# The scores of the RWKV scans: both banks claimed first, the products of the two heads in turn

## The chip, the cores and the metric

The kernel runs on one core of one Trainium2 chip. The metric is the time of one execution on the device, in microseconds (us); the median of three runs counts. A core has TensorE (matrix products, with results in the eight banks of PSUM), VectorE, ScalarE and GpSimd, and queues that issue DMAs.

## The reference

The reference is one inference step of a hybrid trunk: two layers (DEPTH = 2) over 512 latent and 128 context tokens, 1024 channels. Each layer has one input projection whose columns feed four parallel groups (RWKV-7 time mixing, retention, Mamba-2, differential attention), an output projection and a gated ConvFFN. The change lies in the RWKV group, 4 heads of 64 channels and two directions:

```python
def rwkv_scan(r, w, k, v, kk, a, s0):
    def step(s, inp):
        r_t, w_t, k_t, v_t, kk_t, a_t = inp
        sa = jnp.einsum('bhvk,bhk->bhv', s, -kk_t)
        s = s * w_t[:, :, None, :] + sa[..., None] * (kk_t * a_t)[:, :, None, :] + v_t[..., None] * k_t[:, :, None, :]
        return s, jnp.einsum('bhvk,bhk->bhv', s, r_t)
    ...
y_f, s_f = rwkv_scan(rh, hs(decay[:, :, 0]), k_f, vh, kk, hs(a_f), s0[:, 0])
y_b, s_b = rwkv_scan(flip_t(rh), flip_t(hs(decay[:, :, 1])), flip_t(k_b), flip_t(vh), flip_t(kk),
                     flip_t(hs(a_b)), s0[:, 1])
```

## The kernel before

Tokens are on the free axis (642 columns: 512 latent, a gap, 128 context), channels on the 128 partitions. Projections are float32r products in three parts (high and low halves), 48 products per 128 output channels.

The RWKV scan is computed in chunks of 64 tokens, ten in all (eight latent, two context). A tile of 128 channels holds two heads, on partitions 0 to 63 and 64 to 127, so each layer has four passes: tile t = 0, 1 and direction d = 0, 1. A pass has three stages.

- `rw_pre` builds the decayed vectors A and R (`A4`) and B and K (`B2`), and from them the scores: for each chunk e and head h, one product of 64 contraction rows, 128 by 128 in fp32 (line 575). The chunks come in three groups g of 4, 4 and 2 (`GRP`, line 447). A group takes one PSUM bank per head (`SMT`, line 573), so head h works on the row half 64h to 64h + 63 of the array and writes its own bank. VectorE then masks each bank out in two evictions, into `sca` (line 578) and `pk` (line 579), and four copies on ScalarE and GpSimd take the diagonal blocks into `AT` (line 584). `need(g)` (line 570) first drives the pass before until `pk`'s two buffers can be written again.
- `rw_sub` (line 622) inverts the chunks' triangles, a chain of short VectorE steps, with `rhs` (transposes `vt`, `bt`, products `rp`) between.
- `rw_solve` (line 698) makes `y`, the maps (`bg` on TensorE, read into `gq` by lines 732 to 736) and the sequential steps `st`.

Passes overlap: `rw_solve` of one pass runs beside `rw_pre` of the next (lines 1471 to 1484). The stages share four PSUM banks (`sbank`, line 120); a new tile takes a bank whose readers have finished. Projections (`p0r`, `gd` with its conv steps at lines 402 and 403, `rv`, `sx` and others) don't depend on the scan and stand in the same queues.

The order on each engine is not written out. A planner at build time walks all instructions once, with its own reckoning of their durations, and gives each engine at each moment the instruction that is earliest in the source among those whose inputs and tile are ready; on the chip each queue runs in that fixed order. `tc.high_priority` and `tc.issue_after` move a few blocks; none of them stands around the scores.

Further on, in the Mamba-2 group, two banks `pf` (`sf` in the trace) and `pi` (`si`) are claimed together (line 1121) and their products alternate in the source; then come the outputs of retention and attention, the output projection `po`, and the FFN (`pu`, `pd`).

Of the kernel before, what the change touches and what calls it, by code (L numbers as in the profile page):

```python
# [70 lines left out]
def tile_trunk(ctx: ExitStack, tc: tile.TileContext, xT, cT, wmod, win, wv1, wv2, wout, wup, wdn, wlora, gup, pp, srw,  # L71
# [9 lines left out]
    def mm(*a, **k):  # L81
        nonlocal last_pe
        last_pe = nc.tensor.matmul(*a, **k).ins  # L83
# [42 lines left out]
    def SMT(name):  # L126
        return sbank.tile(name)
# [29 lines left out]
    sc = keep.tile([128, KD, 32], F32, name="sc")  # L157
# [340 lines left out]
    def rw_pre(l, t, d, f, wa, rw, dv, S, need):  # L498

        nm = f"{l}_{t}_{d}"  # L500
# [66 lines left out]
        for g, ms in enumerate(GRP):  # L567
            nb = 2 * len(ms)
            n0 = 4 * g
            need(g)  # L570
            pk = rw.tile([128, 2 * len(GRP[g]), 2, 2, 64], F32, tag="pk2" if g == 2 else "pk", name=f"pk{nm}_{g}")
            for h in range(2):
                ps = SMT(f"sc{nm}_{g}_{h}")
                for e in range(nb):
                    mm(ps[:, 128 * e:128 * e + 128], lhsT=B2[64 * h:64 * h + 64, n0 + e, :],
                       rhs=A4[64 * h:64 * h + 64, :, n0 + e, :], start=True, stop=True)
                p4 = ps[:, 0:128 * nb].rearrange("p (e s c) -> p e s c", e=nb, s=2)
                vtt(sca[:, h, n0:n0 + nb], p4[:, :, 0, :], maskA.unsqueeze(1).to_broadcast([128, nb, 64]), MULT)
                vtt(pk[:, 0:nb, h, 1, :], p4[:, :, 1, :], maskR.unsqueeze(1).to_broadcast([128, nb, 64]), MULT)

            at = AT[:, n0:n0 + nb, :].rearrange("p (m h) c -> p h m c", h=2)
            for q in range(4):
                c0 = 32 * (q % 2)
                (nc.scalar.copy if q % 2 else nc.gpsimd.tensor_copy)(
                    at[32 * q:32 * q + 32], sca[32 * q:32 * q + 32, :, n0 + q // 2:n0 + nb:2, c0:c0 + 32])
            pks.append(pk)
            yield
# [786 lines left out]
    for l in range(DEPTH):  # L1374
# [28 lines left out]
        h = (hhi, hlo)  # L1403
# [20 lines left out]
        f = {}  # L1424
# [31 lines left out]
        def need(S_):  # L1456
            def upto(g):
                while S_["maps"] <= g:
                    pump(behind, 1)
            return upto  # L1460

        def pre(i):
            t, d = divmod(i, 2)
            if not d:
                if t:
                    fs[t] = rw_load(t)
                rw_prep(l, t, fs[t], dv, rw)
                yield
            yield from rw_pre(l, t, d, fs[t], wa, rw, dv, Ss[i + 1], need(Ss[i]))
# [414 lines left out]
```

## Time and profile before

| | us |
|---|---|
| median of three runs (2236.89 to 2243.23) | 2240.26 |
| the profiled execution | 2239.36 |
| its span, first to last instruction | 2237.6 |
| TensorE busy | 2098.0 (94%) |
| VectorE busy | 1312.9 (59%) |
| ScalarE busy | 815.2 (36%) |
| GpSimd busy | 275.6 (12%) |
| mean granted TensorE clock | 0.964 |

Engines are named PE (TensorE products), PEld (its weight loads), DVE (VectorE), ACT (ScalarE), POOL (GpSimd) and SP (a DMA queue). L83 is the helper that issues every product, so products are told apart by the tile that they write. An fp32 product has two records on PE. A record's end is modelled, and records of PE overlap: what a run of them costs is read from the starts. In a timeline, rows of the same kind are merged: start, time from the first start to the last end, and how many. The text in brackets is idle time just before, and what ended it.

### The profile page before, as it was taken

What the parts mean: (1) busy time and instruction counts of PE and PEld (TensorE: products, weight loads), DVE (VectorE), ACT (ScalarE), POOL (GpSimd) and SP (SyncE); (2) the same over time, 40 slices, a digit from 0 to 9 for tenths busy, and PEclk for the clock granted to TensorE, in tenths of its full rate; (3) what the DMA queues carried; (4) which work ended last, traced back from release to release, by engine and by line L of the source; (5) the groups of instructions that cost most, each with busy time, mean ns of one, the idle gap of its engine ahead of it and who ended that gap; (6) DMA issues with size and microseconds to landing.
All of it is one profiled execution on the core that took longest, in us unless ns stands there. A gap on an engine that the chain in (4) does not pass through costs nothing. (4 is left out here: it accounts for less than half of the span.)

```text
span 2237.6 us, 40813 instructions
## 1 busy us (share of the span) xinstructions
PE 2098.0 (94%) x16169; PEld 1908.4 (85%) x16169; DVE 1312.9 (59%) x2911; ACT 815.2 (36%) x1603; POOL 275.6 (12%) x460
## 2 busy tenths in 40 slices
PE   6999999987999999999989999999699999999997
PEld 3888887676889999999988888777578899999997
DVE  4787874546665535545457787656376654453553
ACT  4433432225553313323344334232264432232332
POOL 3112122310020000000121121222001100000002
PEclk9999997988999999999989999999799999999998
DMA  7212125664343422222321212265732222222221
GB/s 249 73 51 78 49 83 178 225 194 116 107 146 103 125 76 71 69 78 76 98 82 59 73 58 83 65 231 185 227 104 74 76 75 76 76 72 75 76 70 68
DMA packets 130943, 232.25 MB, mean 104 GB/s; under 512 B 14784, under 2 KB 34752, under 8 KB 130752
## 3 DMA queue, kind: packets, MB, share of 16 engines
q1 hardware_dynamic: 98304, 176.47, 26.3%
q10 hardware_dynamic: 32448, 53.17, 7.1%
q8 instruction: 128, 2.10, 0.4%
q14 instruction: 63, 0.52, 0.1%
HBM read 199.16 MB, written 30.42 MB: 103 GB/s over the span
## 5 line engine op out<-in xcount | busy, mean ns | idle before, releaser
L83 PE MATMUL pu<-hlo_n,wh_up 128*128 128x322 f32 (+1 forms) x1408 | 324.1, 310 | 1.0 <-POOL hlo_n L357 0.7
L83 PE MATMUL pu<-hhi_n,wh_up 128*128 128x322 f32 (+1 forms) x1408 | 323.8, 311 | 0.8 <-DVE gv L403 0.8
L83 PE MATMUL pu<-hhi_n,wl_up 128*128 128x322 f32 (+1 forms) x1408 | 323.6, 310 | 0.0
L184 DVE TENSOR_TENSOR wl_up<-wr_up,wh_up 128x512 fp32r<-128x512 f32 x176 | 124.7, 709 | 250.9 <-ACT wh_up L183 248.0
L83 PEld LDWEIGHTS pu<-hhi_n,wh_up 128*128 128x128 f32 x1408 | 236.8, 189 | 7.0 <-ACT gv L401 2.5
L83 PEld LDWEIGHTS pu<-hlo_n,wh_up 128*128 128x128 f32 x1408 | 236.9, 188 | 2.0 <-POOL hlo_n L357 1.4
L83 PEld LDWEIGHTS pu<-hhi_n,wl_up 128*128 128x128 f32 x1408 | 237.4, 189 | 0.0
L183 ACT CAST wh_up<-wr_up 128x512 fp32r<-128x512 f32 x176 | 108.3, 616 | 297.9 <-PE pu L83 254.0
L83 PE MATMUL pd<-gh,wl_dn 128*128 128x322 f32 x704 | 162.6, 312 | 0.0
L83 PE MATMUL pd<-gh,wh_dn 128*128 128x322 f32 x704 | 162.3, 312 | 0.0
L83 PE MATMUL pd<-gl,wh_dn 128*128 128x322 f32 x704 | 162.1, 311 | 0.0
L183 ACT CAST wh_dn<-wr_dn 128x512 fp32r<-128x512 f32 x96 | 56.0, 584 | 209.6 <-PE pd L83 168.1
L184 DVE TENSOR_TENSOR wl_dn<-wr_dn,wh_dn 128x512 fp32r<-128x512 f32 x96 | 61.9, 645 | 109.9 <-ACT wh_dn L183 109.3
L83 PEld LDWEIGHTS pd<-gh,wh_dn 128*128 128x128 f32 x704 | 119.5, 190 | 0.8 <-ACT gv L401 0.8
L83 PEld LDWEIGHTS pd<-gl,wh_dn 128*128 128x128 f32 x704 | 119.2, 190 | 0.3
L83 PEld LDWEIGHTS pd<-gh,wl_dn 128*128 128x128 f32 x704 | 119.1, 190 | 0.0
L410 DVE SCALAR_TENSOR_TENSOR x<-pd,mod,x 128x512 f32<-128x512 f32 x96 | 48.5, 547 | 93.7 <-PE pd L83 93.7
L83 PE MATMUL po<-ohi,wh_out 128*128 128x320 f32 (+1 forms) x256 | 77.3, 325 | 12.9 <-ACT ohi L198 12.8
L402 DVE SCALAR_TENSOR_TENSOR gv<-pu,pp,gv 128x641 f32<-128x641 f32 x88 | 77.9, 885 | 9.6 <-ACT gv L401 1.9
L403 DVE SCALAR_TENSOR_TENSOR gv<-pu,pp,gv 128x641 f32<-128x641 f32 x88 | 78.0, 887 | 3.2
L401 ACT ACTIVATE gv<-pu,pp 128x642 f32<-128x642 f32 x88 | 77.8, 884 | 0.0
L83 PE MATMUL po<-olo,wh_out 128*128 128x322 f32 (+1 forms) x256 | 77.7, 324 | 0.1
(741 smaller groups left out, 4477.4 us busy)
## 6 DMA issues: line engine op xcount, KB each, us to landing
wr_mod<-in_wmod SPq DMA_DIRECT2D x192, 256.0 KB, 4.8
wr_up<-in_wup SPq DMA_DIRECT2D x176, 256.0 KB, 2.6
wr_dn<-in_wdn SPq DMA_DIRECT2D x64, 256.0 KB, 2.7
wr_dn<-in_wdn SPq DMA_DIRECT2D x32, 192.0 KB, 2.3
olo<-scr_o ACTq DMA_DIRECT2D x16, 321.0 KB, 4.2
wr_out<-in_wout SPq DMA_DIRECT2D x16, 256.0 KB, 2.6
wr_out<-in_wout SPq DMA_DIRECT2D x32, 128.0 KB, 2.1
x_in<-in_xT SPq DMA_DIRECT2D x8, 321.0 KB, 5.7
```

The lines of the kernel that those rows point to most:

```text
L83: last_pe = nc.tensor.matmul(*a, **k).ins
L183: nc.scalar.copy(hi[:, :n], raw[:, :n])
L184: vtt(lo[:, :n], raw[:, :n], hi[:, :n].bitcast(F32), SUB)
L401: act(out, ps, AF.Identity, bias=0.0 if bias is None else bias, scale=wc)
L402: vstt(out[:, 1:T], ps[:, 0:T - 1], wl, out[:, 1:T], MULT, ADD)
L403: vstt(out[:, 0:T - 1], ps[:, 1:T], wr, out[:, 0:T - 1], MULT, ADD)
L410: vstt(xs, halves[0][:, c0:c0 + n], g[:, s:s + 1], xs, MULT, ADD)
```

## The change

Both banks of a group are claimed before its products, and the loops over chunks and heads change places, so that in the source the products of the two heads alternate. The evictions follow in a second loop over the heads, in the order of before. No product, eviction, bank or byte is added or removed.

```diff
             pk = rw.tile([128, 2 * len(GRP[g]), 2, 2, 64], F32, tag="pk2" if g == 2 else "pk", name=f"pk{nm}_{g}")
-            for h in range(2):
-                ps = SMT(f"sc{nm}_{g}_{h}")
-                for e in range(nb):
+            pss = [SMT(f"sc{nm}_{g}_{h}") for h in range(2)]
+            for e in range(nb):
+                for h, ps in enumerate(pss):
                     mm(ps[:, 128 * e:128 * e + 128], lhsT=B2[64 * h:64 * h + 64, n0 + e, :],
                        rhs=A4[64 * h:64 * h + 64, :, n0 + e, :], start=True, stop=True)
+            for h, ps in enumerate(pss):
                 p4 = ps[:, 0:128 * nb].rearrange("p (e s c) -> p e s c", e=nb, s=2)
                 vtt(sca[:, h, n0:n0 + nb], p4[:, :, 0, :], maskA.unsqueeze(1).to_broadcast([128, nb, 64]), MULT)
                 vtt(pk[:, 0:nb, h, 1, :], p4[:, :, 1, :], maskR.unsqueeze(1).to_broadcast([128, nb, 64]), MULT)
```

## Rows read from the trace of the kernel before

**Rows 1.** Stretches: PE, PEld, DVE, ACT, POOL busy (count), PEclk, DMA share, GB/s.

```profile
90.00:300.00 210.00, 203.04 (x2465) 178.50 (x2464) 169.74 (x577) 83.49 (x182) 34.35 (x109) 0.98 0.23 69
...
1191.00:1400.00 209.00, 202.30 (x2468) 177.47 (x2467) 169.19 (x569) 83.86 (x182) 34.70 (x109) 0.99 0.22 69
```

**Rows 2.** Timeline, layer 0, first pass: start, us, engine, line, operation, tiles, count.

```profile
91.78 3.60 PE L83 MATMUL sc<-AR,BK 64*128 64x128 f32 x40 [0.85 <-DVE BK L551]
...
92.36 0.87 DVE L402 SCALAR_TENSOR_TENSOR st_gd<-p0gd,d_muh,st_gd 64x641 f32<-64x641 f32 x1
...
93.16 0.41 DVE L578 TENSOR_TENSOR sca<-sc,cs 128x256 f32<-128x256 f32 x1
...
94.81 0.41 DVE L579 TENSOR_TENSOR pk<-sc,cs 128x256 f32<-128x256 f32 x1
...
95.37 0.96 PE L484 MATMUL vt<-cs,rwv 128*128 128x128 f32 x5
...
98.79 0.88 DVE L403 SCALAR_TENSOR_TENSOR st_gd<-p0gd,d_muh,st_gd 64x641 f32<-64x641 f32 x1
```

**Rows 3.** Timeline, layer 0, second pass, groups 0 and 1.

```profile
136.97 1.16 PE L83 MATMUL sc<-AR,BK 64*128 64x128 f32 x8
...
137.78 0.57 DVE L736 TENSOR_TENSOR gq<-bg,AR 64x128 f32<-64x128 f32 x2
...
138.06 0.39 PE L83 MATMUL rv<-wl_rv,hhi_n 128*128 128x264 f32 x1
...
138.74 1.16 PE L83 MATMUL sc<-AR,BK 64*128 64x128 f32 x8
...
140.37 1.95 PE L83 MATMUL bg<-pk,wx 128*128 128x128 f32 x16
```

**Rows 4.** Timeline of PE from 136.95 to 137.05 us alone.

```profile
136.77 0.28 PE L83 MATMUL bg<-pk,wx 128*128 128x128 f32 x1
136.97 0.37 PE L83 MATMUL sc<-AR,BK 64*128 64x128 f32 x1
```

**Rows 5.** Timeline, same pass, group 2: from 145.9 to 146.0 us alone, and whole.

```profile
145.95 0.39 PE L83 MATMUL sc<-AR,BK 64*128 64x128 f32 x2
...
145.95 0.72 PE L83 MATMUL sc<-AR,BK 64*128 64x128 f32 x8
```

**Rows 6.** Timeline, the pair sf and si of the Mamba-2 group, one instance.

```profile
445.11 0.49 PE L83 MATMUL sf<-css,gb 128*128 128x128 f32 x2
445.53 0.49 PE L83 MATMUL si<-ldsC,sst 64*128 64x128 f32 x2
```

**Rows 7.** Timeline, the same pair, the next instance.

```profile
452.72 0.49 PE L83 MATMUL sf<-css,gb 128*128 128x128 f32 x2
...
453.86 1.16 PE L83 MATMUL si<-ldsC,sst 64*128 64x128 f32 x8 [0.36 <-DVE rpt L952]
```

**Rows 8.** Timeline, layer 1, first pass.

```profile
1193.07 3.60 PE L83 MATMUL sc<-AR,BK 64*128 64x128 f32 x40 [0.72 <-DVE BK L551]
...
1196.66 0.96 PE L484 MATMUL vt<-cs,rwv 128*128 128x128 f32 x5
```

**Rows 9.** Timeline of PE, first and last sf of the same steps, both layers.

```profile
365.31 1.06 PE L83 MATMUL sf<-css,gb 128*128 128x128 f32 x4
...
378.21 0.41 PE L83 MATMUL sf<-css,gb 128*128 128x128 f32 x1
...
1465.28 1.06 PE L83 MATMUL sf<-css,gb 128*128 128x128 f32 x4
...
1473.42 0.38 PE L83 MATMUL sf<-css,gb 128*128 128x128 f32 x2
```

**Rows 10.** Stretches around these steps, columns as in rows 1.

```profile
360.00:370.00 10.00, 7.38 (x35) 6.14 (x34) 7.53 (x7) 2.57 (x6) 5.09 (x4) 0.75 0.72 258
370.00:380.00 10.00, 10.00 (x40) 9.05 (x40) 2.25 (x5) 2.27 (x8) 0.00 (x0) 0.50 0.36 109
...
1470.00:1480.00 10.00, 10.00 (x72) 9.29 (x75) 6.01 (x10) 4.52 (x12) 0.00 (x0) 1.00 0.52 157
```

## The prediction

> **What bounds the kernel now.** I read the stretches first, then the scores' own instructions, then the order of time around them. The scores are made in two stretches, one per layer, 90 to 300 us and 1191 to 1400 us. In both TensorE is busy for 97% (203.04 of 210 us and 202.30 of 209) and VectorE for 81% [rows 1]. So TensorE sets the pace there: the scan's chain runs on VectorE, and projections that don't depend on it fill TensorE between its steps. A saving on TensorE counts nearly in full if the fill can move up into it; a delay on VectorE counts as far as TensorE then runs dry.
>
> The scores are 20 fp32 products for each of 8 passes (layer, tile, direction): 4, 4 and 2 chunks, for two heads. The trace has two records for each product, so a head's four products are "x8". There are two kinds of pass. The first of each layer is one run of 40 records, 3.60 us [rows 2, 8]. In the six others the two heads of a group of four chunks are apart: eight records of one head, other products, eight records of the other [rows 3]. This is so in all 12 such groups; the groups of two chunks are one run of eight [rows 5].
>
> **What the chip does with the two heads now.** Eight records of one head take 1.16 us [rows 3]; less the 0.27 us of the last, 0.89 us for seven steps, the first of which is long because the kind of tile changes. The steady step is that of the whole-array products bg, (1.95 - 0.27)/15 = 0.112 us [rows 3]. The run of eight records that holds both heads takes only 0.72 us, and within 0.05 us of its start two records are under way [rows 5], where a run of one head has one [rows 4]. The code queues head 0's two products ahead of head 1's there, so the two row halves already run side by side when the queue is short: 0.056 us per record. The run of 40 lies between: (3.60 - 0.27)/39 = 0.085 us per record.
>
> The Trainium skill, TensorEngine Tiling (Array Packing), Theoretical Speedup, gives up to 2x where the contraction is 64 or less. By that figure an unpaired run of 40 would go from 40 x 0.112 = 4.5 us to 2.2 us, an estimate. The run measures 3.60 us, so the trace shows that half of this gain is already there. TensorE: Matmul & The Clock Gate, The mechanism, of the same skill says that products start in strict program order; the pair at 145.95 us, queued head after head, differs from that, and the measurement decides.
>
> **The change part by part.** No product, eviction, bank or byte is added or taken away. Both banks of a group are claimed ahead of its products, and the products alternate in the source. What counts is the order in which the planner then puts them.
>
> (a) The 12 separated groups. Head 1's products stand apart because their bank comes free later: head 0 starts at 136.97 and is done by 138.13, VectorE's reads of the older products (gq) end at 137.78 + 0.57 = 138.35, and head 1 starts at 138.74; between them stand four projection products, the first at 138.06 us [rows 3]. The source has nothing between the two heads. The planner passes over a product whose bank isn't free and takes the next one that is ready. The kernel has the same pattern elsewhere: sf and si are claimed together and alternate in the source. Where both banks are free they alternate in the trace, two records each [rows 6]. Where si's bank is not free, all of sf goes first and si follows in one run of eight, after a wait for VectorE [rows 7]. Products of one bank keep their own order, but head 0's second doesn't depend on head 1's first. So in these 12 groups I expect head 0's four, then the fill, then head 1's four: today's order. Cost 0.
>
> Bounds: if they do pair, eight steps of 0.112 us are shared (0.90 us) and one change of tile kind goes: from its start to the next work's a run takes 1.09 us (136.97 to 138.06) where eight steps are 0.90, and it starts 0.20 us after the product ahead of it (136.77 [rows 4]) where a step is 0.11. So a run less saves 1.09 + 0.09 = 1.18 us, and 12 groups 14.2 us.
>
> (b) The six groups of two chunks outside the first passes already run at 0.056 us per record, whichever head is queued first. Cost 0.
>
> (c) The two first passes. All banks are free, so there the order does change: groups 0 and 1 alternate, 32 records at 0.056 instead of 0.085 us, 0.93 us less TensorE per layer, 1.9 us in all. Is it on the path? VectorE evicts from 93.16 us on, at one eviction per 0.33 us ((94.81 - 93.16)/5), with no idle time remarked, because the conv step L402 holds it until 92.36 + 0.87 = 93.23 us [rows 2]. TensorE's next work, vt, takes the bank that the sixth eviction frees: 94.81 + 0.41 = 95.22 us, and vt starts at 95.37 us [rows 2]. So VectorE is the bound of this stretch, and the 0.93 us become a wait of TensorE before vt, or before the last four products, whose banks are freed by the second and fourth evictions, at 93.16 + 0.33 + 0.41 = 93.90 us and 94.56 us. Layer 1 has the same picture: scores 1193.07, vt 1196.66 us [rows 8]. Saved on the path: 0.
>
> What the change costs there: head 0's last product is now the 15th of 16 records instead of the eighth. It ends at 91.78 + 0.1 + 15 x 0.056 + 0.27 = 92.99 us; VectorE can't take it before 93.16 us. The cover is L402. Without any overlap it would end at 91.88 + 15 x 0.112 + 0.27 = 93.83 us, 0.67 us late, 1.3 us for both layers. If the planner reckons this eviction as late and puts the second conv step L403 (0.88 us at 98.79 us [rows 2]) ahead of it, the chain starts 0.88 us later per layer, +1.8 us. So (c) lies between -1.9 and +1.8 us, and I take 0, since the evictions are back to back in the rows.
>
> The sum is 0: 2239.36 us for the profiled execution (span 2237.6 and 1.8 outside it), 0.9 us below the median 2240.26 of the three runs. I forecast 2240 us. A measurement here tells about 0.3%, 6.7 us, from no change.
>
> **Rivals.** First, the heads alternate in all 16 large groups after all: the planner holds both banks first, or frees them earlier in its own reckoning. Then up to 14.2 us of TensorE go at a stage that is 97% TensorE: 2225 us. Against it stand [rows 6, 7]; and head 0's evictions would wait for the later bank (138.35 instead of 138.13 us), so VectorE may keep half: 2232 us. The Theoretical Speedup cited above would be this case.
>
> Second, slower. The plan is made once for the whole program, and the late readiness of head 0 in (c) moves it: L403 goes first, the chain starts 0.88 us later in both layers, and projections fall due at other places behind. The place where that costs is the thin stretch after the scans. The same steps from sf to sf take 378.21 - 365.31 = 12.90 us in layer 0 and 1473.42 - 1465.28 = 8.14 us in layer 1 [rows 9], in the same order; the granted clock was 0.50 in the one (1.2 GHz), after ten us in which TensorE was busy for 7.38, and 1.00 in the other (2.4 GHz) [rows 10]. So such a dip costs 4.8 us. If layer 1 gets it too, 2239.4 + 1.8 + 4.8 = 2246 us; with a second one 2251 us. It decides as soon as TensorE waits longer ahead of 1465 us than now. Third, the same accident the other way: layer 0's dip goes, 2235 us.
>
> **How the numbers follow.** The forecast has 0.71, the first rival 0.12, the slower one 0.12, the third 0.05. Faster by over 0.3% (below 2233.5 us): three quarters of the first rival (0.09; the rest is its half price, at the bound) and 0.03 of a plan that changes for the better. Slower by over 0.3% (above 2247 us): the slower rival with a second dip, half of it (0.06), and 0.04 for more such places than the one I priced. Within 0.3% the rest, 0.78. The range reaches to half of the first rival and to one dip, 2231 to 2247 us, and leaves out its full price and the second dip.
>
> **What would show it.** In the profile after: two runs of 32 or 40 score records, about 0.9 us shorter up to their gap, at the start of each layer, and still VectorE evictions 0.33 us apart behind them; vt no earlier relative to the first eviction. In the other passes, runs of eight with other products between them. If runs of 16 records stand there instead, step (a) is wrong and the time should fall by up to 14 us. If L403 stands ahead of the evictions, or the granted clock differs around 370 and 1470 us, the difference is the plan's and not the pairing's.

## The result, and the profile after the change

The changed kernel took 2252.97 us in the median of nine executions (2248.51 to 2260.24), the kernel before 2237.42 us beside it (nine, 2227.23 to 2243.23). The ratio is 1.0077, with a 95% interval from 1.0057 to 1.0097: 0.8% slower, some 15.5 us. The forecast was 2240 us, with a range from 2231 to 2247. The profiled execution took 2249.32 us, with a span of 2247.6; the one of the kernel before, 2239.36. These two are 10.0 us apart, so the rows below explain 10 us and not all of the 15.5.

The rows of the changed kernel that answer to [rows 2, 3, 5] come first: the timeline of layer 0's first pass, then of its second (start, us, engine, line, operation, tiles, count, idle time before and who ended it). Behind the edit a line number has grown by one: L579 and L580 are the evictions that were L578 and L579.

```profile
91.46 2.06 PE L83 MATMUL sc<-AR,BK 64*128 64x128 f32 x32 [0.85 <-DVE BK L551]
94.32 0.46 PE L83 MATMUL sc<-AR,BK 64*128 64x128 f32 x2 [0.81 <-DVE pk L580]
94.99 0.68 PE L83 MATMUL sc<-AR,BK 64*128 64x128 f32 x6 [0.21 <-DVE pk L580]
...
95.85 0.60 PE L484 MATMUL vt<-cs,rwv 128*128 128x128 f32 x4
...
92.04 0.87 DVE L402 SCALAR_TENSOR_TENSOR st_gd<-p0gd,d_muh,st_gd 64x641 f32<-64x641 f32 x1
92.83 0.68 DVE L184 TENSOR_TENSOR wl_in0k<-wr_in0k,wh_in0k 128x512 fp32r<-128x512 f32 x1
93.43 0.41 DVE L579 TENSOR_TENSOR sca<-sc,cs 128x256 f32<-128x256 f32 x1
93.77 0.41 DVE L580 TENSOR_TENSOR pk<-sc,cs 128x256 f32<-128x256 f32 x1
...
136.12 1.16 PE L83 MATMUL sc<-AR,BK 64*128 64x128 f32 x8
137.20 0.39 PE L83 MATMUL rv<-wl_rv,hhi_n 128*128 128x264 f32 x1
...
137.89 1.16 PE L83 MATMUL sc<-AR,BK 64*128 64x128 f32 x8
...
145.12 0.71 PE L83 MATMUL sc<-AR,BK 64*128 64x128 f32 x8
```

Three things are to be seen. In the first pass the heads take turns: 32 records in 2.06 us. In the second pass nothing has changed: eight records of one head, four projection products, eight of the other. And on VectorE a weight split, L184, has come between the conv step L402 and the first eviction, which now starts 1.97 us after the burst (93.43 - 91.46), against 1.38 us in [rows 2]. Behind it TensorE waits 0.81 us for the evictions, and vt starts 4.39 us after the burst (95.85 - 91.46) instead of 3.59 (95.37 - 91.78).

The 0.59 us would not make 15. But the split is only the first of many places that differ. Compared instruction by instruction, the planner gave another place to 3286 of 13417 products on TensorE, 846 of 2775 instructions on VectorE and 407 of 1743 on ScalarE. All of them lie in the first 315 us behind a layer's first score, of some 555 up to its first up product; from there on the two programs run in one order again.

Where the time went shows in the stretches. First the changed kernel, in the columns of [rows 1] (length; busy time of PE, PEld, DVE, ACT, POOL; granted clock; DMA): the two score stretches, the thin stretch of both layers, and each layer from its first score to its first up product.

```profile
90.00:300.00 210.00, 202.09 (x2465) 177.80 (x2464) 169.35 (x577) 83.78 (x182) 37.25 (x108) 0.98 0.23 69
1191.00:1400.00 209.00, 201.46 (x2466) 177.01 (x2467) 168.50 (x566) 83.65 (x181) 37.84 (x109) 0.99 0.22 69
370.00:380.00 10.00, 10.00 (x65) 8.75 (x65) 5.80 (x10) 4.22 (x12) 0.54 (x1) 1.00 0.50 132
1460.00:1470.00 10.00, 6.17 (x35) 5.57 (x33) 2.10 (x5) 2.06 (x5) 4.38 (x4) 0.78 0.93 349
1470.00:1480.00 10.00, 10.00 (x35) 8.04 (x35) 2.18 (x4) 1.93 (x6) 0.67 (x1) 0.50 0.35 99
...
91.46:650.38 558.92, 510.73 (x4516) 429.99 (x4516) 374.46 (x1036) 210.58 (x485) 101.86 (x168) 0.94 0.38 119
1191.30:1754.71 563.41, 516.49 (x4514) 434.84 (x4514) 376.45 (x1024) 210.77 (x484) 101.45 (x176) 0.93 0.37 116
```

The kernel before, in rows of the same view that were not shown:

```profile
91.78:651.15 559.37, 514.47 (x4515) 435.02 (x4516) 376.36 (x1038) 210.89 (x485) 97.84 (x168) 0.93 0.38 119
1193.07:1744.86 551.79, 506.29 (x4514) 427.93 (x4515) 374.19 (x1022) 210.76 (x484) 98.66 (x176) 0.95 0.38 119
1460.00:1470.00 10.00, 7.69 (x42) 6.64 (x41) 7.53 (x8) 3.29 (x9) 5.22 (x4) 0.83 0.72 257
```

Layer 0 took 0.45 us less than before and layer 1 11.62 us more. Layer 0 had lost 2.6 us by its last gated output (gg), and had them back by its first up product: its low-clock dip at 370 us [rows 10] was gone, 1.00 there now. Layer 1 had lost 3.8 us at the same point, and then the dip came to it, after ten us in which TensorE was busy for 6.17 instead of 7.69: 0.50 at 1470 us, where [rows 10] has 1.00.

One execution has its dips where another has none, so I read the granted clock of all of them. Twenty executions of the kernel before (beside the first experiments) have mean clocks of 0.959 to 0.968, and their times fall along a line by 1.8 us for each 0.001; one more ran in a slow state, 2322.5 us at a clock of 0.833, and is left out. At 0.962 the kernel before took 2240.4 to 2242.9 us (four executions) and the changed one 2249.3 (one), and the nine of the changed kernel lie 7.7 us above that line in the mean: some 8 us at an equal clock. The mean clock fell from 0.964 to 0.960, which is worth 7 more by the same line.

### The profile page after: what moved, and what is told of

The parts are those of the page before. It is cut to its first block, busy times and chain, and to the rows that moved or that the text cites. A ratio compares the mean times of both kernels' runs of the same rounds, so it can differ in the third digit from the quotient of the medians.

```text
span 2247.6 us, 40797 instructions
## 1 busy us (share of the span) xinstructions
PE 2103.4 (94%) x16169; PEld 1909.9 (85%) x16169; DVE 1313.2 (58%) x2911; ACT 815.1 (36%) x1603; POOL 282.5 (13%) x460
## 5 line engine op out<-in xcount | busy, mean ns | idle before, releaser
L83 PE MATMUL pu<-hlo_n,wh_up 128*128 128x322 f32 (+1 forms) x1408 | 324.1, 310 | 0.9 <-POOL hlo_n L357 0.9
L83 PE MATMUL pu<-hhi_n,wh_up 128*128 128x322 f32 (+1 forms) x1408 | 324.0, 311 | 0.8 <-DVE gv L403 0.8
L83 PE MATMUL pu<-hhi_n,wl_up 128*128 128x322 f32 (+1 forms) x1408 | 323.6, 310 | 0.0
L184 DVE TENSOR_TENSOR wl_up<-wr_up,wh_up 128x512 fp32r<-128x512 f32 x176 | 124.7, 710 | 250.8 <-ACT wh_up L183 248.0
L83 PEld LDWEIGHTS pu<-hhi_n,wh_up 128*128 128x128 f32 x1408 | 237.0, 189 | 7.3 <-ACT gv L401 2.5
L83 PEld LDWEIGHTS pu<-hlo_n,wh_up 128*128 128x128 f32 x1408 | 236.9, 188 | 1.6 <-POOL hlo_n L357 1.4
L83 PEld LDWEIGHTS pu<-hhi_n,wl_up 128*128 128x128 f32 x1408 | 237.4, 189 | 0.0
L83 PE MATMUL pd<-gh,wl_dn 128*128 128x322 f32 x704 | 162.6, 312 | 0.0
L83 PE MATMUL pd<-gh,wh_dn 128*128 128x322 f32 x704 | 162.3, 312 | 0.0
L83 PE MATMUL pd<-gl,wh_dn 128*128 128x322 f32 x704 | 162.1, 311 | 0.0
L184 DVE TENSOR_TENSOR wl_dn<-wr_dn,wh_dn 128x512 fp32r<-128x512 f32 x96 | 61.9, 645 | 109.9 <-ACT wh_dn L183 109.3
L83 PEld LDWEIGHTS pd<-gh,wh_dn 128*128 128x128 f32 x704 | 119.5, 190 | 0.8 <-ACT gv L401 0.8
L83 PEld LDWEIGHTS pd<-gl,wh_dn 128*128 128x128 f32 x704 | 119.2, 190 | 0.3
L83 PEld LDWEIGHTS pd<-gh,wl_dn 128*128 128x128 f32 x704 | 119.1, 190 | 0.0
L83 PE MATMUL po<-ohi,wh_out 128*128 128x320 f32 (+1 forms) x256 | 77.4, 325 | 13.1 <-ACT ohi L198 13.1
L402 DVE SCALAR_TENSOR_TENSOR gv<-pu,pp,gv 128x641 f32<-128x641 f32 x88 | 77.9, 885 | 9.6 <-ACT gv L401 1.9
L403 DVE SCALAR_TENSOR_TENSOR gv<-pu,pp,gv 128x641 f32<-128x641 f32 x88 | 78.0, 886 | 3.1
L83 PE MATMUL po<-olo,wh_out 128*128 128x322 f32 (+1 forms) x256 | 78.0, 325 | 0.0
```

The costliest lines, as they stand in the source:

```text
L184: vtt(lo[:, :n], raw[:, :n], hi[:, :n].bitcast(F32), SUB)
L402: vstt(out[:, 1:T], ps[:, 0:T - 1], wl, out[:, 1:T], MULT, ADD)
L403: vstt(out[:, 0:T - 1], ps[:, 1:T], wr, out[:, 0:T - 1], MULT, ADD)
```

## The experiments

Three theories. **Order:** the planner's new order of the whole stage costs the time, and the products themselves nothing. **Local:** the first eviction's 0.6 us and the wait of TensorE behind it are passed down the chain. **Products:** taking turns costs, on TensorE or in the banks.

In several of these kernels a list of places is held with edges that make one instruction follow another on its own engine, without a wait. The list (`seq`) names instructions by their number in the source's order; a -1 parts two lists. It needs the names of all instructions, so a helper records every operation there, and the profile puts all of them on L83.

### Products and order parted

The first kernel has the old products and the new order. One edge is enough for it: the split L184 is held ahead of the first eviction in each layer, and the planner does the rest.

```diff
-        vtt(lo[:, :n], raw[:, :n], hi[:, :n].bitcast(F32), SUB)
+        i_ = vtt(lo[:, :n], raw[:, :n], hi[:, :n].bitcast(F32), SUB).ins
+        if name in ("in0k1_1", "in1k1_1"):
+            tc.add_manual_dep(sca0, i_.name, mybir.DependencyInfo(mybir.DependencyClass.NoSync, mybir.DependencyReason.DATA), reason="seed")
...
-            for e in range(nb):
-                for h, ps in enumerate(pss):
+            for e, h in ([(e, h) for e in range(nb) for h in range(2)] if False else
+                         [(e, h) for h in range(2) for e in range(nb)]):
+                for ps in (pss[h],):
```

> The products go head after head again, as in the kernel before, in all 16 groups; but the weight split that stands ahead of the first eviction in the changed kernel is held there by an edge on VectorE, and with that the planner gives every engine the order of the changed kernel (only 40 places on TensorE differ, the products inside the bursts; VectorE, ScalarE and SyncE have none). Theory plan (the loss is the planner's new order, not the products): 2253 us as in the changed kernel, at least 2249. Theory products (taking turns costs by itself, on TensorE or in the banks): 2237 us, as before. Mixed: in between, and the two shares can be read off together with the next kernel.

Measured: 2253.54 us, ratio to the kernel before 1.0059 (1.0036 to 1.0082). The second kernel has the new products in the old order: edges along 140 places on TensorE, 30 on VectorE and 8 on ScalarE behind each layer's burst bring the rest back too. The lists themselves are left out here:

```diff
...
+        seq = [int(v) for v in seq.split(",")]
+        for a, b in zip(seq, seq[1:]):
+            if min(a, b) > 0:
+                tc.add_manual_dep(seen[f"I-{b}"], f"I-{a}", mybir.DependencyInfo(
+                    mybir.DependencyClass.NoSync, mybir.DependencyReason.DATA), reason="order")
```

> The products take turns as in the changed kernel (in the two first passes and in the six groups of two chunks), but edges on TensorE, VectorE and ScalarE behind the first burst of each layer keep the order of the kernel before; only the 40 places inside the bursts differ from it. Theory plan: 2237 us, as before, within 0.2%; the forecast's own cost of the change (0 for its steps, bounds -1.9 to +1.8 us) is tested by this kernel. Theory products: 2253 us. First eviction after the burst's start: 1.4 us if head 0 is still done before VectorE comes free, as the forecast had it.

Measured: 2242.2 us, ratio 1.0000 (0.9979 to 1.0022). Its first pass on the timeline:

```profile
91.79 2.06 PE L83 MATMUL sc<-AR,BK 64*128 64x128 f32 x32 [0.85 <-DVE BK L83]
...
95.38 0.96 PE L83 MATMUL vt<-cs,rwv 128*128 128x128 f32 x5
...
92.38 0.87 DVE L83 SCALAR_TENSOR_TENSOR st_gd<-p0gd,d_muh,st_gd 64x641 f32<-64x641 f32 x1
93.18 0.40 DVE L83 TENSOR_TENSOR sca<-sc,cs 128x256 f32<-128x256 f32 x1
...
94.83 0.40 DVE L83 TENSOR_TENSOR pk<-sc,cs 128x256 f32<-128x256 f32 x1
```

TensorE's 32 records take the same 2.06 us as in the changed kernel, but the first eviction starts 1.39 us after the burst, as in [rows 2] (1.38), and vt at 95.38 against 95.37. So the theory of the products falls in both kernels, and the loss goes with the order, within the intervals.

These two kernels also part the order from the low-clock dips of a single profile. First the kernel with the old order, in the columns of [rows 1], then the one with the new order:

```profile
360.00:370.00 10.00, 7.12 (x40) 6.43 (x38) 7.52 (x7) 2.57 (x6) 5.20 (x5) 0.83 0.66 236
370.00:380.00 10.00, 10.00 (x70) 9.24 (x70) 5.61 (x10) 4.72 (x12) 0.00 (x0) 1.00 0.56 167
1460.00:1470.00 10.00, 7.20 (x37) 6.11 (x36) 7.52 (x7) 2.63 (x7) 5.20 (x4) 0.83 0.73 260
1470.00:1480.00 10.00, 10.00 (x72) 9.60 (x73) 6.10 (x10) 4.72 (x12) 0.00 (x0) 1.00 0.51 152
```

```profile
370.00:380.00 10.00, 10.00 (x36) 8.04 (x36) 2.84 (x5) 2.09 (x6) 1.20 (x1) 0.50 0.31 98
```

With the old order the granted clock from 370 us on is 1.00, where the kernel before has 0.50, though TensorE was busy for less of the ten us ahead (7.12 against 7.38). It stays at 1.00 from 1470 us on too, after 7.20 us instead of 7.69. With the new order it is 0.50 from 370 us on, where the changed kernel has 1.00. So where a dip falls in one profile isn't a mark of the order.

### The first eviction by itself

```diff
+        with tc.issue_after(last_pk) if name in ("in0k1_1", "in1k1_1") else ExitStack():
             vtt(lo[:, :n], raw[:, :n], hi[:, :n].bitcast(F32), SUB)
...
+        with tc.issue_after(last_pk) if M == 64 else ExitStack():
             vstt(out[:, 0:T - 1], ps[:, 1:T], wr, out[:, 0:T - 1], MULT, ADD)
```

> The changed kernel, with the weight split and the gate's third convolution step held behind the first two pairs of evictions on VectorE: VectorE then goes from the second convolution step to the first eviction as in the kernel before, but further on the planner keeps the changed kernel's order (some 3296 places on TensorE against 3286). Theory local (the 0.6 us by which the first eviction comes later, and the wait of TensorE behind it, is what is lost, passed down the chain): the RWKV stage is back at the length before, and the time at about 2240 us. Theory plan (the first eviction's delay is nothing, the order of the whole stage behind it counts): within 0.2% of the changed kernel, 2249 to 2256 us.

Measured: 2256.46 us, ratio 1.0076 (1.0057 to 1.0095). VectorE in its first pass:

```profile
92.44 0.87 DVE L403 SCALAR_TENSOR_TENSOR st_gd<-p0gd,d_muh,st_gd 64x641 f32<-64x641 f32 x1
93.23 0.40 DVE L581 TENSOR_TENSOR sca<-sc,cs 128x256 f32<-128x256 f32 x1
```

The burst starts at 91.86 there, so the first eviction is on time (1.37 us) and the loss is all there. The local theory falls. It also shows that the split's place doesn't set the order by itself: here it stands behind the evictions, and the planner's order is the changed kernel's all the same, but for 210 products on TensorE. With the old products the split's place was enough. That in both the planner reckons the first eviction as later is argued; no run shows its reckoning.

### One layer at a time

The turns are taken in layer 1 alone, and in the second kernel, with `l == 0`, in layer 0 alone:

```diff
-            for e in range(nb):
-                for h, ps in enumerate(pss):
+            for e, h in ([(e, h) for e in range(nb) for h in range(2)] if l == 1 else
+                         [(e, h) for h in range(2) for e in range(nb)]):
+                for ps in (pss[h],):
```

> The products take turns in layer 1 alone; layer 0 has products and order of the kernel before. From the landmarks of the two profiles layer 0 lost 2.9 us up to its gated outputs and had it back by the up products (its low-clock dip went away), layer 1 lost 3.4 us and then 8 more (the dip came there). Theory each layer by itself: layer 1 carries the loss, 2237 + 11.6 = 2249 us, at least 2247. Theory that the dip of layer 1 hangs on what layer 0 did before (its phase or the clock's history): the dip stays in layer 0, layer 1 loses 3 to 4 us alone, 2241 us.

> The products take turns in layer 0 alone; layer 1 has products and order of the kernel before. Layer 1 alone cost 11 us of the 15.5. If the layers add up: 2237.7 + 4.5 = 2242 us. If layer 0 costs nothing of its own (by the landmarks of the changed kernel's trace it had lost nothing by its up products): 2237 to 2238 us. If each layer's loss depends on the other's: more than 2246 us.

Measured: layer 1 alone 2248.76 us, ratio 1.0046 (1.0031 to 1.0062); layer 0 alone 2241.23 us, ratio 1.0022 (1.0005 to 1.0038). Together 0.68%, within the errors of the changed kernel's 0.77%: the layers add up. My reading of the landmarks, that layer 0 costs nothing, was wrong by the times, and by little. Single profiles don't show this cost: layer 0 took 558.92 us in the changed kernel's and 559.55 in that of layer 0 alone, against 559.37 before.

### Another order of the same work

The edges of the kernel with the old order, but fewer: in each layer the lists stop after 80 places instead of 140 on TensorE, 16 instead of 30 on VectorE and 4 instead of 8 on ScalarE.

> Same products as in the changed kernel, but edges hold only the first 80 places on TensorE and 16 on VectorE behind the first burst of each layer at the order of the kernel before; from there the planner goes a third way (3580 places on TensorE differ from the kernel before, and most of them from the changed kernel too). If the changed kernel's order is a bad one by itself (its 8 us earlier retention values, say), this one has no reason to share the loss: 2237 us. If the order of the kernel before is a rare good one and other orders of the same work cost what the changed one costs, 2247 to 2260 us.

Measured: 2251.56 us, ratio 1.0072 (1.0046 to 1.0098). A third order costs as much as the changed kernel's, by another way: its last gated output comes 265.4 us after layer 0's first score, against 254.6 before and 257.2 in the changed kernel. Here too the first eviction comes late, 1.98 us after the burst.

### Turns in all 16 groups

In the 12 groups that the planner keeps apart, edges now hold the products in turn. The lists give TensorE the old order, with head 0's products moved down to head 1's place, and in the next kernel head 1's moved up. The trace follows the old order in this way up to 288 us in layer 0; behind that, and on VectorE from 139 us on, the planner went its own way. In all, 904 products on TensorE and 504 instructions on VectorE have another place than in the kernel before. So this is a fourth order and not the old one. At the first group of the second pass the two lists read as follows, the minus line in the first kernel, the plus line in the next (1454 to 1461 are the scores in turn, 3028 to 3031 the projection rv):

```diff
-1446, 3028, 3029, 3030, 3031, 1454, 1455, 1456, 1457, 1458, 1459, 1460, 1461, 1471
+1446, 1454, 1455, 1456, 1457, 1458, 1459, 1460, 1461, 3028, 3029, 3030, 3031, 1471
```

> Edges make TensorE follow the order of the kernel before through the whole RWKV stage, but with the products of all 16 groups of a layer pair taking turns: in the 12 groups that stay head after head in the changed kernel, head 0's products are moved down to where head 1's stand. First rival of the forecast (turn-taking saves 1.18 us of TensorE for each of the 12 groups): 2237 - 14.2 = 2223 us, at most 2230. Against it: head 0's evictions then start up to 1.8 us later, and VectorE, which is busy for 169.7 of 210 us in this stretch, hands them on later: TensorE's busy time falls by some 7 us a layer, its waits rise by as much, and the time stays within 0.3% of 2237 us.

> As the kernel with all pairs, but head 1's products are moved up to where head 0's stand. If only the length of the runs on TensorE counts, the same time as that kernel. If it is the banks (head 1's bank is not free when head 0's products start, so that all TensorE waits for an eviction), slower than it by up to 1.2 us a group, 14 us in all: 2237 us or more; a wait in front of the pairs shows it.

Measured: 2220.01 us, ratio 0.9930 (0.9909 to 0.9951), and 2226.42 us, ratio 0.9957 (0.9939 to 0.9975). The first comes near the sum of the forecast's first rival (2225), and is faster than the kernel before and the changed one. Its rows made me doubt the reason: the timeline of the second pass, and from the groups of the score products who ended TensorE's idle time (us, times).

```profile
137.29 0.49 PE L83 MATMUL sc<-AR,BK 64*128 64x128 f32 x2
138.33 1.13 PE L83 MATMUL sc<-AR,BK 64*128 64x128 f32 x14 [0.56 <-ACT wx L83]
139.38 0.71 PE L83 MATMUL y<-R,GG 128*128 128x128 f32 x4
...
253.49 1.16 PE L83 MATMUL sc<-AR,BK 64*128 64x128 f32 x16
254.58 0.82 PE L83 MATMUL bg<-pk,wx 128*128 128x128 f32 x5
```

```profile
  ACT wx L83: 2.6, 6
...
  DVE gq L83: 1.5, 4
```

The same of the kernel with head 1 moved up:

```profile
136.77 0.48 PE L83 MATMUL sc<-AR,BK 64*128 64x128 f32 x2
138.30 1.13 PE L83 MATMUL sc<-AR,BK 64*128 64x128 f32 x14 [1.04 <-ACT wx L83]
```

```profile
  ACT wx L83: 10.7, 10
...
  ACT st_sx L83: 1.6, 2
```

Head 0's first product runs, then TensorE waits for head 1's bank, which ScalarE (wx, st_sx) or VectorE (gq) sets free: 4.1 us in ten of the twelve groups, and 12.3 us in all twelve with head 1 moved up. That kernel is 6 us slower, but its order on VectorE is another one too. With head 0 moved down, the group at 137 us takes 2.09 us up to the next work (137.29 to 139.38). Two runs of eight behind one another would take 1.09 + 0.90 = 1.99 us by [rows 3]. Only in the last group of four of each layer is head 1's bank free in time; there the turns bring what the rival counted on, 16 records in 1.09 us (253.49 to 254.58). So the turns can't have brought the 16 us, and the next kernel parts them again: the old products in the same order on VectorE, ScalarE and SyncE, and on TensorE but for the bursts (on GpSimd 16 of 460 instructions change places in the trace).

```diff
-            for e in range(nb):
-                for h, ps in enumerate(pss):
+            for h, ps in enumerate(pss):
+                for e in range(nb):
```

> The order of the kernel with all pairs on every engine (TensorE differs in 112 places, all inside the bursts; VectorE, ScalarE and SyncE in none), but in every group head 0's products come first and head 1's behind them, in one run. In the kernel with all pairs most of the 12 groups' bursts lasted 1.9 to 2.2 us, with a wait for head 1's bank after the first two records, where two runs of eight behind one another would take about 2.0 us (1.09 for the first run to the next start, 0.9 for eight records more): so the turns themselves gain little there, and the gain of 15.8 us may be another order's. Theory order: 2220 us again, at most 2226. Theory turns (1.18 us a group saved by the pairs): 2234 us or more.

Measured: 2217.97 us, ratio 0.9924 (0.9901 to 0.9947), the fastest of all. The timeline of its second pass with the group that answers to the one at 253 us, and its two layers:

```profile
137.16 2.16 PE L83 MATMUL sc<-AR,BK 64*128 64x128 f32 x16
139.26 0.71 PE L83 MATMUL y<-R,GG 128*128 128x128 f32 x4
...
252.06 1.71 PE L83 MATMUL sc<-AR,BK 64*128 64x128 f32 x16
253.69 1.05 PE L83 MATMUL bg<-pk,wx 128*128 128x128 f32 x7
```

```profile
91.50:633.91 542.41, 500.10 (x4516) 423.69 (x4516) 377.00 (x1038) 210.55 (x485) 97.83 (x168) 0.96 0.40 123
1175.39:1723.38 547.99, 505.63 (x4515) 426.75 (x4515) 373.26 (x1024) 210.51 (x484) 98.52 (x176) 0.95 0.39 120
```

The group at 137 us takes 2.1 us with or without turns, the one at 252 us 1.63 us without (252.06 to 253.69) against 1.09 with; all twelve take 21.8 us with turns and 22.9 without, up to the next work each, where the kernel before has 24 runs of 1.08 us (26.0). The two layers together take 20.8 us less than in the kernel before (1111.16 to 1090.40). This gain, too, is the order's. Some 4 us of it can be the merging of two runs into one (26.0 - 22.9, and 0.09 us less in front of each of 12), an estimate; what brings the rest stays open. Last, turns in all groups with everything else left to the planner, which is what the words of the change describe. Only the groups stand in the lists:

```diff
+1454, 1455, 1456, 1457, 1458, 1459, 1460, 1461, -1, 1502, 1503, 1504, 1505, 1506, 1507, 1508, 1509, -1
```

> Only inside each group of eight are the products held in turn by edges; where the groups stand, and all else, is left to the planner (3756 places on TensorE differ from the kernel before, 3154 from the changed kernel). This is the change as its words describe it. Theory turns: 14 us below the changed kernel, 2239 us or less. Theory order: anything that the orders seen so far gave, 2220 to 2256 us, and the RWKV stage's length (its last gated output at 254.6 us after the first burst in the kernel before, 257.2 in the changed one, 255.1 with all pairs in the old order, 265.4 in the third order) tells which.

Measured: 2240.96 us, ratio 1.0023 (1.0006 to 1.0040). Its second pass:

```profile
135.93 0.49 PE L83 MATMUL sc<-AR,BK 64*128 64x128 f32 x2
136.34 0.39 PE L83 MATMUL rv<-wl_rv,hhi_n 128*128 128x264 f32 x1
...
137.75 1.16 PE L83 MATMUL sc<-AR,BK 64*128 64x128 f32 x14
```

Here the planner fills the wait for head 1's bank with projections. TensorE's work gets shorter, but it runs ahead with fill that isn't due: 254 us after layer 0's first score the trace has 20 records of the projection rg (p0rg), of which the kernel before has none, and the last gated output comes 4 us later (258.5 against 254.6). The time is 12 us below the changed kernel's, near what the theory of turns said (2239); but 3154 products on TensorE have another place than there, so this pair can't tell turns from order.

### Half an order

Where in the order is the loss? Both kernels have the changed kernel's products. The one follows the new order in each layer up to the third pass's solve and the old one behind it, the other the reverse. The lists on TensorE begin:

```diff
+805, 1219, 827, 828, 829, 830, 1220, 1221, 834, 1222, 1223, 1224, 846
...
+805, 827, 828, 829, 830, 834, 1219, 1220, 846, 847, 848, 849, 860
```

> The changed kernel's products; in each layer TensorE, VectorE and ScalarE follow the changed kernel's order from the first burst to the third pass's solve (some 140 us), and from there what is left is in the order of the kernel before. In the profiles of before and after the third solve starts 2.1 and 2.5 us later relative to the first burst, the last gated output 2.6 and 3.8 us, the first up product of layer 1 11.6 us. Theory first part (the chain of the scans falls behind in the first 140 us, and the rest only passes this on and adds the clock): 2253 us as the changed kernel. Theory second part (the places behind the third solve cost): 2237 to 2241 us. Adding up: its loss and that of the next kernel give 15.5 us together.

> The other half: the order of the kernel before from the first burst to the third pass's solve, the changed kernel's order behind it. Theory first part: 2237 us, as before. Theory second part: 2250 us or more. If the orders of two halves that were made for one another cost more when parted, both this and the kernel before it are slower than either whole order.

Measured: new, then old 2246.72 us, ratio 1.0043 (1.0021 to 1.0066); old, then new 2249.86 us, ratio 1.0059 (1.0040 to 1.0078). Each half costs, and the two together 1.0%, which the intervals don't part from the whole new order's 0.8%. So the loss isn't at one place, unless the parting of two halves costs by itself, which these kernels can't tell. What each place costs stays open.

### What the orders did to TensorE

For the two layers from the first score to the first up product, one execution of each kernel, worked out from its trace: TensorE's idle time, and the busy time that went to the low clock (busy time times one minus the granted clock, in stretches of 5 us). The column "rest" is what remains of the length; by the kernels without turns in all groups (970.5 to 978.1) it is good to some 4 us.

| kernel | length | idle | low clock | rest | median us |
|---|---|---|---|---|---|
| before | 1111.2 | 90.4 | 45.8 | 975.0 | 2237.4 |
| changed | 1122.3 | 95.1 | 51.0 | 976.2 | 2253.0 |
| old products, new order | 1125.4 | 97.1 | 50.2 | 978.1 | 2253.5 |
| new products, old order | 1116.2 | 90.2 | 52.1 | 973.9 | 2242.2 |
| the eviction first | 1131.9 | 97.1 | 61.1 | 973.7 | 2256.5 |
| third order | 1131.3 | 101.6 | 54.1 | 975.6 | 2251.6 |
| all in turn, head 0 down | 1094.1 | 91.3 | 36.8 | 966.0 | 2220.0 |
| the order of "head 0 down", no turns | 1090.4 | 84.7 | 34.0 | 971.7 | 2218.0 |
| all in turn, head 1 up | 1102.5 | 100.5 | 36.7 | 965.4 | 2226.4 |
| all in turn, planner's order | 1112.6 | 99.6 | 45.2 | 967.8 | 2241.0 |

The four kernels that aren't listed (turns in one layer, half an order) lie between: 91.9 to 96.6 us idle, 43.4 to 54.7 of low clock, 970.5 to 974.6 of rest. In the one order that was run with and without them, turns in all groups take some 6 us of work off TensorE (971.7 to 966.0), and its idle time grows by as much (84.7 to 91.3). The kernels differ by up to 17 us of idle time and 27 us of low clock, and little in the rest but for the turns. Of the low clock some 6 us is one execution's chance: the kernel before and the one with its order and new products differ by that much. Over all their executions the mean granted clock does go with the order: 0.964 for both kernels of the old order, 0.960 and 0.961 for both of the new one, 0.969 to 0.971 for both of "head 0 down". Why one order leaves TensorE more idle than another stays open.

## Why the prediction was wrong

- **(a) The 12 separated groups stay as they are: right.** Runs of eight with other products between them, as in [rows 3].
- **(b) The groups of two chunks: right**, 0.71 us at 145.12 against 0.72 in [rows 5].
- **(c) The first passes, cost 0: right for the products, wrong for the kernel.** With the old order held, the ratio is 1.0000 (0.9979 to 1.0022), the records take the forecast 0.056 us ((2.06 - 0.27)/31 = 0.058), and vt stands where it stood, 3.59 us after the burst. The term's bounds, -1.9 to +1.8 us, are finer than that interval.
- **The step that failed is the cover in (c), and with it the taking of the order as given.** "VectorE can't take it before 93.16 us. The cover is L402" is true of the chip as long as the old order is held: the first eviction then comes 1.39 us after the burst. But the planner made another order: a split stands ahead of head 0's eviction, and 3286 products on TensorE have another place. The sum went over the operations that the edit moves, and put the moved order at nothing. The runs showed that the order alone is the loss: 1.0059 with the old products, 1.0000 with the new products in the old order.
- **The slower rival had the mechanism in part, and too small a price.** It said that the late readiness of head 0 moves the plan: other work first on VectorE, projections elsewhere. The moved plan is shown; that the late readiness moved it is argued. It named L403 (0.88 us) where L184 came (0.68 us, which put the eviction off by 0.59). Its first term, the eviction's delay, was worth nothing that could be told: the kernel with the eviction on time lost as much. Its second term, a dip in layer 1 for 4.8 us, is seen in the profiled execution, but that is luck: the other kernel with the new order has such a dip in layer 0 (0.50 from 370 us on). And its condition (TensorE waits longer ahead, so the clock falls) fails in layer 1 of the kernel with the old order, where TensorE was busy for 7.20 us instead of 7.69 and the clock behind was 1.00. The rival gave 2246 us, with a second dip 2251; the measured 2253 lies beyond. Its chance was 0.12. What it had no term for is the order itself, some 8 us at an equal clock, and the lower mean clock, some 7.
- **The base was 3 us high.** The forecast stood on three executions of the kernel before (2240.26 us); nine have 2237.42. This is small beside the miss.
- **The first rival's price came out by luck.** 2225 us was its sum and 2220 was measured where all groups take turns in an order held by edges; but without turns that order gives 2218. What the turns save there, the wait for head 1's bank takes; the rival's price for a group is seen only in the two groups where that bank was free.
- **One sign does not hold.** "If L403 stands ahead of the evictions, or the granted clock differs around 370 and 1470 us, the difference is the plan's": the clock differs at both places, but it also differs at 370 us between two kernels of one order. The sign that held is the work ahead of the evictions, L184 in place of L403.

## What to carry to other kernels

Where a planner makes the order of a whole program, price an edit twice: by its operations, and by the order that it sets loose. Ask whether any instruction becomes ready later in the planner's reckoning at a moment when its engine is free; if so, the spread of orders (here 2218 to 2254 us for the same products, head after head) is part of the range. Before one credits or blames an edit, hold the order and change the edit, then hold the edit and change the order: here the first moved nothing that could be told in three pairs of kernels, and the second up to 1.4% (0.9924 to 1.0059 with the old products).

## What the hardware showed that I had not expected

- The granted clock of one and the same program varies from one execution to the next, 0.959 to 0.968 in twenty of the kernel before, and with it the time, 2229 to 2248 us. A single profile's dips say little on a change of this size.
- A head's product that waits for its bank holds up the other head's that stand behind it: in the kernel with head 1 moved up, TensorE stood idle for 1.04 us at 137 us, and for up to 1.77 us elsewhere, in front of 14 records, six of them head 0's, whose bank was free.
